# The split operands hhi, hlo, thi and tlo start 128 bytes later in every partition

## The chip, the cores and the metric

The kernel runs on one core of a Trainium2 chip. The metric is the device time of one execution in microseconds (us), taken as the median of 3 runs: 2562.43 us before the change (2559.01 to 2567.07).

TensorE multiplies, VectorE (DVE) and ScalarE (ACT) do the element-wise work, GpSimd (POOL) and SyncE (SP) mostly start transfers. The on-chip memory SBUF has 128 partitions. A tile has the same start in each of them, counted in bytes from the start of a partition; this document calls that number its address.

## The reference

Two layers of a decoder trunk work on a sequence of 1024 tokens with a model width of 1024, in float32. Each layer does, in this order:

```
h = rms_norm(x, norm1_w[l]) * (1.0 + sc1) + sh1
x = x + g1 * hybrid_mixer(h, w_in[l], w_out[l], ...)
h = rms_norm(x, norm2_w[l]) * (1.0 + sc2) + sh2
x = x + g2 * conv_ffn(h, w_gate[l], w_val[l], conv_w[l], conv_b[l], w_down[l])
```

The six vectors sh1 to g2 come from `silu(c) @ ada_w[l] + ada_b[l]`. The mixer projects h to 4096 columns, runs four retention heads and four gated linear recurrence (HGRN2) heads of 128 columns each, and projects back. Its lower bounds are `cumsum(softmax(hgrn_lb_logits)) - p[0]`, a handful of numbers per head. The gated MLP has 2816 columns and a causal convolution of width 3 on its gate branch. A last rms_norm ends it.

## The kernel before, in words

Every large product keeps float32 accuracy by splitting each operand in two numbers of the type float32r, a high and a low one, and adding three products: high by high, high weight by low operand, low weight by high operand. One such triple is lines 453 to 455 (`product`), 528 to 530 (`slot_mm`) or 368 to 370 (`gemm_half`). Each multiplication takes a weight tile of 128 x 128 and streams a moving tile of 128 x 512.

The moving tiles lie in four buffers. `hhi` and `hlo` hold the normalised input (2 halves x 8 slices x 512 columns each) or, in later stages, other operands; `thi` and `tlo` hold three sets of 4 slices for the Strassen-like scheme of `pair`, which makes the product of two blocks in seven multiplications of 4 triples. The weights arrive by DMA in `raw`, are split by ACT (line 330, `whi`) and DVE (line 331, `wlo`), and sit in six buffers of each kind. The moving buffers are filled by ACT (the high part: lines 311, 323, 414 and 533) and DVE (the low part: lines 312, 324, 415 and 534), most often from one of the twelve general tiles `z`.

Over the whole kernel there are 9360 of these 512-column multiplications: 5712 in `pair` (68 pairs of 84), 768 in plain units, 768 for the output projection `wo` and 2112 for `w_down`. Beside them TensorE does transposes and the small attention products, in plain float32 on tiles `z`.

The order of the work comes from the order in which the code is written and from priorities given to the scheduler. Addresses have no part in it. They come from the order in which a pool's tiles are asked for: each starts where the one before it ended, rounded up to 32 bytes. The pool `const` starts at 16512 and holds the twelve `z`, `ident`, `onec`, `hhi`, `hlo`, then small constants. Among these are `lbc`, `omlb`, `ex` and `sm`, 32 bytes each, which the function `bounds` fills once and the HGRN2 heads read as per-partition scalars. The pool `tops` opens when the input buffers of the start (`boot`) are given back, and takes their place from 179680 on: first a tile `shift` that nothing reads or writes, then `thi` and `tlo`.

Of the kernel before, what the change touches and what calls it, by code (L numbers as in the profile page):

```python
# [9 lines left out]
F32 = mybir.dt.float32  # L10
# [6 lines left out]
P = 128  # L17
# [3 lines left out]
DEPTH = 2  # L21
HEADS = 4
# [18 lines left out]
def kernel(  # L41
# [11 lines left out]
    const = ctx.enter_context(tc.tile_pool(name="const", bufs=1))  # L53
# [29 lines left out]
    onec = const.tile([P, 1], F32, name="onec")  # L83
    V.memset(onec, 1.0)

    hhi = const.tile([P, 2, KT, HALF], F32R, name="hhi")
    hlo = const.tile([P, 2, KT, HALF], F32R, name="hlo")
    b11, b12 = (hhi[:, 0, 0:4, :], hlo[:, 0, 0:4, :]), (hhi[:, 1, 0:4, :], hlo[:, 1, 0:4, :])
# [5 lines left out]
    def open_tops():  # L94
        boot.close()
        pool = ctx.enter_context(tc.tile_pool(name="tops", bufs=1, reuse_waits="tile"))
        pool.tile([P, 48], F32, name="shift")
        thi = pool.tile([P, 3, 4, HALF], F32R, name="thi")
        tlo = pool.tile([P, 3, 4, HALF], F32R, name="tlo")
        for i in range(3):  # L100
            tops[i + 1] = (thi[:, i], tlo[:, i])
# [669 lines left out]
    load_cols(1, vec_a, nc.scalar, zc)  # L771
    load_cols(2, vec_b, nc.scalar, zc)
    zc.free()
    lbc = const.tile([P, DEPTH * HEADS], F32, name="lbc")
    omlb = const.tile([P, DEPTH * HEADS], F32, name="omlb")
    ex = const.tile([P, DEPTH * HEADS], F32, name="ex")
    sm = const.tile([P, 8], F32, name="sm")
    first.turn()
    first.keep()
    ada_first(2)  # L780
# [4 lines left out]
    def start_units():  # L785
# [15 lines left out]
        ada_first(3)  # L801
        ada_first(1)
        open_tops()
        st.append(wcols(*parts[2], early=nc.sync))
        part(2, 0, lo)
# [342 lines left out]
```

## Time and profile before

| | |
|---|---|
| median of 3 runs | 2562.43 us |
| the profiled execution's own time | 2557.94 us |
| its span, first to last instruction | 2556.2 us |
| TensorE busy with multiplications | 2483.7 us, 97% of the span |
| TensorE loading weights | 2060.0 us, 81% |
| DVE busy | 1842.0 us, 72% |
| ACT busy | 999.5 us, 39% |
| mean granted TensorE clock | 0.986 of full speed |

The busy time of TensorE counts an instruction from its start to its modelled end, and one starts before the last has ended. So the time between two starts tells more than the duration of one.

### The profile page before, as it was taken

To read this page: it belongs to the slowest core of one execution; us is meant where nothing else is said; L and a number is where in the kernel's file an instruction comes from. 1 tells how busy PE (TensorE), PEld (TensorE's weight loads), DVE (VectorE), ACT (ScalarE), POOL (GpSimd) and SP (SyncE) were. 2 spreads that over 40 slices of the span, in tenths; PEclk is the share of its full clock that TensorE was granted. 3 is DMA by queue.
4 is the path that set the end of the run, shared out by engine and by line. 5 is a ranking of instruction groups with operands and counts; after the bars stand their busy time and mean duration, and the time that the engine had idled before them with its cause. 6 is when DMAs were issued, how large, how long until landed. Compare 5 with 4: busy or idle time off the path is not lost.

```text
span 2556.2 us, 32084 instructions
## 1 busy us (share of the span) xinstructions
PE 2483.7 (97%) x12189; PEld 2060.0 (81%) x12189; DVE 1842.0 (72%) x3045; ACT 999.5 (39%) x1685; POOL 78.3 (3%) x150
## 2 busy tenths in 40 slices
PE   6989999999999999999999999999999999999998
PEld 5778888778888888788888888887878888878887
DVE  6978888755988888734379788776398777773435
ACT  5533443434533333412264443344263333341224
POOL 0000000010000000000000000000000000000000
PEclk8989999999999999999999999999999999999999
DMA  8232332552234435733231211235212222264313
GB/s 306 66 104 83 99 108 72 181 181 79 83 124 148 140 124 165 252 111 97 86 114 58 67 59 42 67 99 161 87 58 83 75 91 83 75 215 133 97 56 109
DMA packets 293916, 283.52 MB, mean 111 GB/s; under 512 B 10794, under 2 KB 240770, under 8 KB 293762
## 3 DMA queue, kind: packets, MB, share of 16 engines
q1 hardware_dynamic: 275904, 219.42, 28.1%
q0 software_dynamic: 17408, 61.88, 6.7%
q8 instruction: 96, 1.57, 0.3%
q14 instruction: 59, 0.48, 0.1%
q10 hardware_dynamic: 449, 0.17, 0.0%
HBM read 229.00 MB, written 52.43 MB: 110 GB/s over the span
## 4 chain that ended last, share of the span: by engine, by line
PE 65%; issue 23%; DVE 5%; DMA 4%; ACT 1%; POOL 0%; SPq 0%; POOLq 0%; ACTq 0%; DVEq 0%
PE f L455 9%; PE f L453 9%; PE f L454 9%; PE dn L530 5%; PE dn L528 5%; PE dn L529 5%; PE wo L529 2%; PE wo L528 2%; PE wo L530 2%; PE dn_last L530 1%; PE dn_last L528 1%; PE dn_last L529 1%; DMA rawwo<-in_w_out_dram 1%; PE g L455 1%; PE g L454 1%
## 5 line engine op out<-in xcount | busy, mean ns | idle before, releaser
L455 PE MATMUL f<-hhi,wlof 128*128 128x512 f32 x640 | 251.6, 393 | 0.0
L453 PE MATMUL f<-hhi,whif 128*128 128x512 f32 x640 | 250.7, 392 | 0.6 <-DVE z L486 0.6
L454 PE MATMUL f<-hlo,whif 128*128 128x512 f32 x640 | 249.8, 390 | 0.0
L486 DVE TENSOR_TENSOR z<-z,f 128x512 f32<-128x512 f32 x240 | 164.2, 685 | 102.5 <-PE f L455 90.4
L455 PE MATMUL f<-thi,wlof 128*128 128x512 f32 x480 | 188.7, 393 | 0.0
L453 PE MATMUL f<-thi,whif 128*128 128x512 f32 x480 | 187.8, 391 | 0.0
L454 PE MATMUL f<-tlo,whif 128*128 128x512 f32 x480 | 187.3, 390 | 0.0
L530 PE MATMUL dn<-hhi,wlodn 128*128 128x512 f32 x384 | 151.9, 396 | 7.7 <-DVE wlodn L331 7.7
L528 PE MATMUL dn<-hhi,whidn 128*128 128x512 f32 x384 | 150.9, 393 | 0.0
L529 PE MATMUL dn<-hlo,whidn 128*128 128x512 f32 x384 | 150.3, 391 | 0.0
L919 DVE SCALAR_TENSOR_TENSOR z<-dn,mod,z 128x512 f32<-128x512 f32 x64 | 48.0, 750 | 134.5 <-PE dn L530 134.5
L454 PEld LDWEIGHTS f<-hlo,whif 128*128 128x128 f32 x640 | 120.2, 188 | 27.2
L453 PEld LDWEIGHTS f<-hhi,whif 128*128 128x128 f32 x640 | 120.2, 188 | 26.2 <-issue 0.9
L455 PEld LDWEIGHTS f<-hhi,wlof 128*128 128x128 f32 x640 | 120.2, 188 | 25.8
L168 DVE SCALAR_TENSOR_TENSOR ac<-aw,cact,ac 128x512 f32<-128x512 f32 x140 | 104.7, 748 | 23.6 <-DMA aw<-in_ada_w_dram 22.6
L330 ACT ACTIVATE whidn<-rawdn 128x512 fp32r<-128x512 f32 x64 | 39.6, 628 | 182.9 <-PE dn L529 171.3
L454 PEld LDWEIGHTS f<-tlo,whif 128*128 128x128 f32 x480 | 90.1, 188 | 20.6
L455 PEld LDWEIGHTS f<-thi,wlof 128*128 128x128 f32 x480 | 90.2, 188 | 19.3
L453 PEld LDWEIGHTS f<-thi,whif 128*128 128x128 f32 x480 | 90.2, 188 | 19.1
L530 PEld LDWEIGHTS dn<-hhi,wlodn 128*128 128x128 f32 x384 | 72.5, 189 | 24.2 <-DVE wlodn L331 8.5
L723 PEld LDWEIGHTS lh<-z,z 128*128 128x128 f32 x640 | 80.4, 198 | 10.6 <-issue 5.3
L529 PEld LDWEIGHTS dn<-hlo,whidn 128*128 128x128 f32 x384 | 72.5, 189 | 16.6
(659 smaller groups left out, 6348.3 us busy)
## 6 DMA issues: line engine op xcount, KB each, us to landing
aw<-in_ada_w_dram SPq DMA_DIRECT2D x160, 256.0 KB, 3.0
acts<-z POOLq DMA_DIRECT2D x44, 512.0 KB, 2.9
z<-acts SPq DMA_DIRECT2D x44, 512.0 KB, 4.3
z<-xd POOLq DMA_DIRECT2D x32, 512.0 KB, 5.8
rawdn<-in_w_down_dram SPq DMA_DIRECT2D x32, 512.0 KB, 4.3
xd<-z POOLq DMA_DIRECT2D x52, 256.0 KB, 2.7
rawdn_last<-in_w_down_dram SPq DMA_DIRECT2D x32, 384.0 KB, 3.6
af<-in_ada_w_dram SPq DMA_DIRECT2D x16, 512.0 KB, 9.8
```

Source lines behind the costliest of these rows:

```text
L168: V.scalar_tensor_tensor(out=a, in0=raw, scalar=cact[:, k:k + 1], in1=a, op0=ALU.mult, op1=ALU.add)
L330: A.activation(hi[:, 0:n], src, AF.Copy)
L453: T.matmul(ps, wh, rh, start=first and k == 0, stop=False, skip_group_check=True)
L454: T.matmul(ps, wh, rl, start=False, stop=False, skip_group_check=True)
L455: T.matmul(ps, wl, rh, start=False, stop=k == 3, skip_group_check=True)
L486: V.tensor_add(o, x, y)
L528: T.matmul(ps, a, rh, start=i == 0, stop=False)
L529: T.matmul(ps, a, rl, start=False, stop=False)
L530: T.matmul(ps, b, rh, start=False, stop=i == last)
L723: T.matmul(ps[:, c * 64:(c + 1) * 64].rearrange("p (b t) -> p b t", t=s), k.t[:, cs], qp.t[:, cs].rearrange("p (b t) -> p b t", t=s)[:, 1: ...
L919: V.scalar_tensor_tensor(out=x, in0=ps, scalar=mod[:, l * 48 + gate + d:][:, 0:1], in1=x, op0=ALU.mult, op1=ALU.add)
```

## The change

```
@@ -83,6 +83,10 @@
     onec = const.tile([P, 1], F32, name="onec")
     V.memset(onec, 1.0)
 
+    lbc = const.tile([P, DEPTH * HEADS], F32, name="lbc")
+    omlb = const.tile([P, DEPTH * HEADS], F32, name="omlb")
+    ex = const.tile([P, DEPTH * HEADS], F32, name="ex")
+    sm = const.tile([P, 8], F32, name="sm")
     hhi = const.tile([P, 2, KT, HALF], F32R, name="hhi")
     hlo = const.tile([P, 2, KT, HALF], F32R, name="hlo")
@@ -94,7 +98,7 @@
         pool = ctx.enter_context(tc.tile_pool(name="tops", bufs=1, reuse_waits="tile"))
-        pool.tile([P, 48], F32, name="shift")
+        pool.tile([P, 80], F32, name="shift")
         thi = pool.tile([P, 3, 4, HALF], F32R, name="thi")
         tlo = pool.tile([P, 3, 4, HALF], F32R, name="tlo")
@@ -771,10 +775,6 @@
     zc.free()
-    lbc = const.tile([P, DEPTH * HEADS], F32, name="lbc")
-    omlb = const.tile([P, DEPTH * HEADS], F32, name="omlb")
-    ex = const.tile([P, DEPTH * HEADS], F32, name="ex")
-    sm = const.tile([P, 8], F32, name="sm")
     first.turn()
```

Four constants of 32 bytes are asked for earlier, and the unused tile grows from 192 to 320 bytes. The table shows the addresses that follow, in bytes, and what is left of them after division by 128, 256, 512 and 1024.

| tile | address before | after | mod 128 | mod 256 | mod 512 | mod 1024 |
|---|---|---|---|---|---|---|
| hhi | 66208 | 66336 | 32, 32 | 160, 32 | 160, 288 | 672, 800 |
| hlo | 98976 | 99104 | 32, 32 | 160, 32 | 160, 288 | 672, 800 |
| thi | 179872 | 180000 | 32, 32 | 160, 32 | 160, 288 | 672, 800 |
| tlo | 204448 | 204576 | 32, 32 | 160, 32 | 160, 288 | 672, 800 |
| cact, mod, modA, cols0 to cols2 | 131744 to 133152 | 128 more | | | | |
| lbc, omlb, ex, sm | 133152 to 133280 | 66208 to 66336 | | | | |
| z0 to z11, ident | 16512 to 66176 | the same | 0 | 128 | 128 | 128 |
| raw, whi, wlo, aw, s1, ac | 134752 to 177760 | the same | 96 | 96 | 96 | 608 |

Slices of the moving buffers are 2048 bytes apart and slices of the weights 512 bytes, so all slices of a buffer have the same remainder by 512. All other tiles stay where they were, and the instructions, their order on every engine and their waits are the same in both kernels, apart from addresses.

## Rows read from the trace of the kernel before

**Rows 1.** The head of the profile page: the span, and each engine's busy time, its share of the span and its number of instructions.

```profile
span 2556.2 us, 32084 instructions
...
PE 2483.7 (97%) x12189; PEld 2060.0 (81%) x12189; DVE 1842.0 (72%) x3045; ACT 999.5 (39%) x1685; POOL 78.3 (3%) x150
```

**Rows 2.** The chain of work that ended last, its shares of the span by engine.

```profile
PE 65%; issue 23%; DVE 5%; DMA 4%; ACT 1%; POOL 0%; SPq 0%; POOLq 0%; ACTq 0%; DVEq 0%
```

**Rows 3.** Busy time of each engine in chosen stretches (us from the start): length, then busy us and number of instructions of PE, PEld (weight loads), DVE, ACT and POOL, the granted clock, the DMA share and GB/s.

```profile
34.00:36.60 2.60, 2.60 (x7) 1.98 (x6) 2.50 (x9) 2.57 (x6) 0.00 (x0) 0.50 1.05 384
...
1900.00:2200.00 300.00, 300.00 (x1312) 246.14 (x1312) 230.56 (x326) 116.41 (x168) 7.97 (x15) 1.00 0.25 80
```

**Rows 4.** TensorE's instructions in order of time, from a stretch at full clock in the output projection: start in us, duration in us, instruction.

```profile
1800.14 0.39 PE L530 MATMUL wo<-thi,wlowo 128*128 128x512 f32 x1
1800.37 0.39 PE L528 MATMUL wo<-thi,whiwo 128*128 128x512 f32 x1
1800.60 0.39 PE L529 MATMUL wo<-tlo,whiwo 128*128 128x512 f32 x1
...
1802.89 0.39 PE L530 MATMUL wo<-thi,wlowo 128*128 128x512 f32 x1
```

**Rows 5.** Groups of TensorE's multiplications, shapes kept apart: line, names, shapes, count, busy us and mean ns of one, idle time before them. They are the largest groups of each moving buffer.

```profile
L455 PE MATMUL f<-hhi,wlof 128*128 128x512 f32 x640 | 251.6, 393 | 0.0
L453 PE MATMUL f<-hhi,whif 128*128 128x512 f32 x640 | 250.7, 392 | 0.6 <-DVE z L486 0.6
L454 PE MATMUL f<-hlo,whif 128*128 128x512 f32 x640 | 249.8, 390 | 0.0
L455 PE MATMUL f<-thi,wlof 128*128 128x512 f32 x480 | 188.7, 393 | 0.0
L453 PE MATMUL f<-thi,whif 128*128 128x512 f32 x480 | 187.8, 391 | 0.0
L454 PE MATMUL f<-tlo,whif 128*128 128x512 f32 x480 | 187.3, 390 | 0.0
```

**Rows 6.** Groups of DVE, the same columns as rows 5. They differ in the buffers that they read and write.

```profile
L331 DVE TENSOR_TENSOR wlodn<-rawdn,whidn 128x512 fp32r<-128x512 f32 x64 | 43.7, 686 | 41.5 <-ACT whidn L330 41.5
L324 DVE TENSOR_TENSOR hlo<-z,hhi 128x512 fp32r<-128x512 f32 x52 | 35.0, 689 | 0.6
L415 DVE TENSOR_TENSOR tlo<-z,thi 128x512 fp32r<-128x512 f32 x48 | 32.8, 690 | 0.1
L432 DVE TENSOR_TENSOR z<-z,z 128x512 f32<-128x512 f32 x16 | 11.0, 690 | 0.0
L312 DVE SCALAR_TENSOR_TENSOR hlo<-t,mod,hhi 128x512 fp32r<-128x512 f32 x12 | 8.5, 748 | 0.0
L207 DVE SCALAR_TENSOR_TENSOR z<-af,cact,z 128x512 f32<-128x512 f32 x28 | 20.9, 747 | 0.0
L534 DVE TENSOR_TENSOR tlo<-z,thi 128x1024 fp32r<-128x1024 f32 x32 | 38.8, 1222 | 15.6 <-ACT thi L533 15.6
L534 DVE TENSOR_TENSOR hlo<-z,hhi 128x1024 fp32r<-128x1024 f32 x28 | 34.0, 1222 | 18.8 <-ACT hhi L533 18.6
L903 DVE TENSOR_TENSOR z<-z,z 128x1024 f32<-128x1024 f32 x16 | 19.6, 1222 | 4.9 <-ACT z L902 3.2 <-DMA z<-md 1.7
```

**Rows 7.** Groups of ACT, the same columns.

```profile
L330 ACT ACTIVATE whidn<-rawdn 128x512 fp32r<-128x512 f32 x64 | 39.6, 628 | 182.9 <-PE dn L529 171.3 <-DMA rawdn<-in_w_down_dram 9.7 <-PE dn L530 1.0
L323 ACT ACTIVATE hhi<-z 128x512 fp32r<-128x512 f32 x52 | 31.7, 624 | 0.6
L414 ACT ACTIVATE thi<-z 128x512 fp32r<-128x512 f32 x48 | 29.3, 628 | 10.6 <-DVE z L433 6.0 <-DVE z L430 4.0 <-DVE z L432 0.2
L533 ACT ACTIVATE thi<-z 128x1024 fp32r<-128x1024 f32 x32 | 33.5, 1059 | 30.2 <-DMA z<-acts 27.8 <-DVE z L903 1.4 <-PE g L455 0.6
L902 ACT ACTIVATE z<-z 128x1024 f32<-128x1024 f32 x16 | 16.9, 1059 | 6.3 <-DVE z L486 6.2
```

**Rows 8.** TensorE's instructions in order of time, the columns of rows 4, near the start, in the stretch of the first line of rows 3, at half clock.

```profile
34.07 0.63 PE L370 MATMUL uh_0f<-hhi,wloh_0f 128*128 128x512 f32 x1
34.50 0.63 PE L368 MATMUL uh_0f<-hhi,whih_0f 128*128 128x512 f32 x1
...
36.63 0.63 PE L368 MATMUL uh_0q<-hhi,whih_0q 128*128 128x512 f32 x1
```

**Rows 9.** The view and columns of rows 8, for two runs of plain float32 multiplications whose operands lie at other addresses: in kvh both are tiles z, in rb the moving tile is rTs (address 177888) and the weights are ident. Rows of one kind are merged: the duration is that of all of them together.

```profile
170.21 1.73 PE L555 MATMUL kvh<-z,z 128*128 128x128 f32 x14
46.15 1.12 PE L293 MATMUL rb<-rTs,ident 4*128 4x128 f32 x8 [0.46 <-DVE rTs L288]
```

**Rows 10.** The durations of one record of the two kinds in rows 9, over the whole run, from the views of the tiles kvh and rb: count, then minimum, median and maximum in ns, first and last start in us.

```profile
L555 PE MATMUL kvh<-z,z x112: 275/275/377, 170.2 to 1675.1; 128*128 128x128 f32 x112
...
L293 PE MATMUL rb<-rTs,ident x64: 270/270/421, 19.4 to 1870.4; 4*128 4x128 f32 x64
```

**Rows 11.** Weight loads of TensorE, the same columns as rows 5.

```profile
L453 PEld LDWEIGHTS f<-hhi,whif 128*128 128x128 f32 x640 | 120.2, 188 | 26.2 <-issue 0.9
L723 PEld LDWEIGHTS lh<-z,z 128*128 128x128 f32 x640 | 80.4, 198 | 10.6 <-issue 5.3 <-DVE z L715 1.3 <-PE h L455 1.2
```

More of the change, by code (lines that the diff above doesn't have):

```diff
@@ L84 @@
     V.memset(onec, 1.0)
+    lbc = const.tile([P, DEPTH * HEADS], F32, name="lbc")
+    omlb = const.tile([P, DEPTH * HEADS], F32, name="omlb")
+    ex = const.tile([P, DEPTH * HEADS], F32, name="ex")
+    sm = const.tile([P, 8], F32, name="sm")
     hhi = const.tile([P, 2, KT, HALF], F32R, name="hhi")
@@ L96, in open_tops @@
         pool = ctx.enter_context(tc.tile_pool(name="tops", bufs=1, reuse_waits="tile"))
-        pool.tile([P, 48], F32, name="shift")
+        pool.tile([P, 80], F32, name="shift")
         thi = pool.tile([P, 3, 4, HALF], F32R, name="thi")
@@ L773 @@
     zc.free()
[L774 to L777, printed above, removed]
     first.turn()
```

## The prediction

> **What bounds the kernel now.** I read the head of the page first. TensorE is busy for 97% of the span, DVE for 72%, ACT for 39% [rows 1]. The chain that ended last says the same in another way: 65% of it is TensorE's own work and 23% is "issue", where the engine waits for nothing that the profile shows, while DVE has 5% and DMA 4% [rows 2]. So the time is set by how fast TensorE takes its instructions, hardly by anyone it waits for. The table by stretches makes this sharper: in the 300 us from 1900 on there is no idle time, the granted clock is 1.00, and 1312 multiplications run [rows 3]. They start 300 / 1312 = 0.2287 us apart. The order in time, from another stage, gives (1802.89 - 1800.14) / 12 = 0.229 us between starts [rows 4]. The "mean ns" of 390 to 393 [rows 5] is a duration with an overlapping end, and the reader should not multiply by it.
>
> This step of 229 ns matters because there are 9360 of these 512-column multiplications: 9360 x 0.229 = 2143 us, 84% of the span of 2556.2. All of them stream a moving tile from hhi, hlo, thi or tlo. The change touches nothing but where these four buffers start, so the question is whether the step of 229 ns hangs on that. One nanosecond per step is 9.36 us.
>
> **The change, part by part.** It removes no instruction, adds none, moves none and adds no wait; SP's and POOL's queues hold the same transfers to the same places, since no transfer writes a tile that moved. What changes is addresses, and each user of a moved tile is a term.
>
> The four constants lbc, omlb, ex and sm, and the columns behind hlo: they are operands of one number per partition, or tiles of at most 108 columns written once. I put them at nothing. Should one of these small accesses cost more, it is DVE's or ACT's, and both stand idle for a good part of the span [rows 1].
>
> DVE and ACT filling the four buffers: here the trace does show several places. DVE's subtraction takes 686 ns where source, second source and result lie in the weight buffers (all 96 mod 256), 689 and 690 ns where they lie in z (128) and the moving buffers (160), and 690 ns where all lie in z [rows 6]. The form with a scalar takes 748 ns with t (96) and hhi (160), 747 with af (224) and z (128). With 1024 columns it is 1222 for thi, for hhi and for z alone. ACT takes 628 for a weight buffer, 624 for hhi, 628 for thi, and 1059 for thi and for z with 1024 columns [rows 7]. These rows differ by at most 0.7%, and the larger one isn't tied to a place. The distances between operands that they show, modulo 256, are 0, 32, 64 and 96; the new distance between z and hhi is 160, which no row has. If it cost another 0.7%, DVE's splits of rows 6 (35.0 + 32.8 + 8.5 + 38.8 + 34.0 = 149 us) would grow by 1 us, beside TensorE's work. Term: 0, bounds -1 and +1 us.
>
> TensorE reading the moving tiles: the one large term. What can the trace say? Of the address modulo 1024, hhi and thi have the same remainder (672), so that rows of hhi and of thi agree to within 3 ns [rows 5] says only that the bits above that do not matter. Remainders modulo 512 other than 160 never occur for these multiplications, so the new place is not shown. Three things bear on it.
>
> First, at half clock (0.50 of 2.4 GHz, so 1.2 GHz [rows 3]) the step is (36.63 - 34.07) / 6 = 0.4267 us [rows 8], which is 512 cycles of 1.2 GHz: one column per cycle and nothing on top. At full clock the columns alone are then half of that, 213.3 ns, and the step of 229 carries 15.6 ns more. If the place of the operand caused this excess, and the new place caused none, the change would be worth 9360 x 15.6 ns = 146 us. That is the bound below.
>
> The Trainium skill puts a number on the same step: its page "TensorE: Matmul & The Clock Gate", section "Wait — 56ns, not 53.3ns?", states 512 columns at full clock as 512 / 2.4 plus about 2.5 ns, 215.7 measured. The trace does not agree: 229. If the page's step were to be had by another address, the gain would be 9360 x 13.3 = 124 us (an estimate from the page), and if it holds for other operand types only, nothing.
>
> Second, plain float32 multiplications with other places: kvh, where weights and moving tile are both z and so have a distance of 0 modulo 256, starts every (1.73 - 0.275) / 13 = 0.112 us. For rb, whose moving tile (177888, so 224 modulo 256) lies 96 from its weights (128), I get (1.12 - 0.27) / 7 = 0.121 [rows 9], with the median of one record taken off as the tail [rows 10]. The difference, 9 ns, is the most that a row shows between two places, and rb has four partitions only and starts after an idle time, which alone may explain it. Taken as it is and per instruction, 9360 x 9.4 ns = 88 us, the bound above.
>
> Third, the weight loads: 188 ns where the weights are float32r (whif), 198 where they are z [rows 11]; both fit in 229, so the load would have to grow by 41 ns before it set the step.
>
> I take 0 for this term, nearest to the rows of DVE and ACT, which read the same buffers at the same places. The excess appears at 2.4 GHz and is absent at 1.2 GHz with the very same addresses, so it looks like a limit on how fast things are taken, not like a collision.
>
> **The sum.** 0 us on the execution of 2557.94 us (span 2556.2 and 1.7 around it). The median of the three runs is 2562.43, 4.5 above it, so the unchanged time to forecast is the median: 2562 us. The three runs span 8 us, and about 0.3%, 7.7 us, is what a measurement of this kernel can tell from no change; it is 0.82 ns per step. The forecast's own range is 2552 to 2572.
>
> **Rivals.**
>
> A, the excess goes: the new place (32 modulo 256 in place of 160) spares some of the 15.6 ns, as a read that meets fewer collisions with the weights would. For it: the excess is unexplained, and of the four places modulo 512 that leave 32 modulo 128 only one was seen. Against it: the step is the same 229 for all four weight slices and for hhi as for thi. Anything from 0.82 to 15.6 ns is open; half of it, 7.8 ns, makes 73 us: 2489 us.
>
> B, the slow side: the moving read and the weight load that runs beneath it come into each other's way at a distance of 192 bytes modulo 512 where they did not at 64. Its place is every one of the 9360 steps, and it decides from 0.82 ns per step. For it: weight loads run through 81% of the span [rows 1], so the two reads are always on at once, and rb's 9 ns. Against it: kvh at distance 0, where the operands should meet most, is the quicker one [rows 9]. Half of rb's difference, 4.7 ns, makes 44 us: 2606 us.
>
> The Trainium skill speaks against both: "SBUF — State Buffer", section "Who interferes with whom", lets only DVE and GpSimd share a port and says that TensorE never waits on anyone. No run here has shown it for another place.
>
> C, DVE or ACT becomes dearer at distance 160 and TensorE is held up. For it: DVE is 72% busy. Against it: rows 6 and 7. At 0.7% of 149 us it would give 2563 us, which is the forecast again.
>
> **How the numbers follow.** Forecast 0.54, A 0.27, B 0.19, with C inside the forecast. Of the forecast I leave 0.02 to a median that falls low by chance and 0.01 to one that falls high: faster by over 0.3% 0.29, within 0.3% 0.51, slower 0.20. For 8 in 10 the range must take in about half of A and of B: down by 9360 x 8.3 ns = 78 us, up by 9360 x 5.3 ns = 50 us, so 2484 to 2612. With gains of all sizes up to 15.6 ns alike likely this holds 0.53 of A, and 0.57 of B up to 9.4 ns.
>
> **What would show it.** Right: in the stretch from 1900 to 2200 us again about 1312 multiplications with no idle time, f, dn and wo at 390 to 396 ns, starts 0.229 us apart at full clock and 0.427 at half. A shows itself as more than 1316 in such a stretch, B as fewer than 1307 (0.82 ns is 0.36% of a step). C would leave the step at 0.229 and show DVE's rows L324, L415 and L534 longer and TensorE idle behind them. The forecast is wrong if the step is anything but 229, since no other term has weight.

## The result and the profile after

The changed kernel takes 2588.63 us (median of 4 runs, 2588.16 to 2589.55) against 2560.72 for the kernel before on the same chip (4 runs, 2558.01 to 2567.07): 1.0106 times as long, 95% interval 1.0086 to 1.0126. So 128 bytes of layout cost 27.9 us. The forecast was no change; the time lies inside the range, on the side of rival B.

The head of the page, the chain's shares and the stretch from 1900 us on, as in [rows 1], [rows 2] and [rows 3]:

```profile
span 2586.4 us, 32084 instructions
...
PE 2520.2 (97%) x12189; PEld 2060.0 (80%) x12189; DVE 1847.3 (71%) x3045; ACT 999.6 (39%) x1685; POOL 78.8 (3%) x150
...
PE 51%; issue 39%; DMA 4%; DVE 4%; ACT 1%; POOL 1%; SPq 0%; POOLq 0%; ACTq 0%; DVEq 0%
```

```profile
32.00:35.00 3.00, 3.00 (x9) 2.28 (x8) 2.93 (x8) 2.97 (x7) 0.00 (x0) 0.50 1.06 387
1900.00:2200.00 300.00, 300.00 (x1287) 241.72 (x1286) 231.50 (x327) 116.91 (x170) 7.98 (x15) 1.00 0.24 78
```

The whole loss stands in the first line: TensorE's busy time grew by 2520.2 - 2483.7 = 36.5 us, while the time in which it did not multiply fell from 72.5 (2556.2 - 2483.7) to 66.2 us. The span grew by the difference, 30.2 us. The stretch without idle time shows where it sits: 1287 multiplications in 300 us in place of 1312, 0.2331 us from one to the next in place of 0.2287, at the same full clock. In the chain, TensorE's own work and "issue" make 90% together, where they made 88% before; only the split between the two is another. TensorE's instructions in order of time, at full clock and in the stretch at half clock near the start, as in [rows 4] and [rows 8]:

```profile
1830.20 0.40 PE L532 MATMUL wo<-hhi,whiwo 128*128 128x512 f32 x1
1830.44 0.39 PE L533 MATMUL wo<-hlo,whiwo 128*128 128x512 f32 x1
...
1833.71 0.39 PE L532 MATMUL wo<-thi,whiwo 128*128 128x512 f32 x1
```

```profile
32.73 0.63 PE L374 MATMUL uh_0f<-hhi,wloh_0f 128*128 128x512 f32 x1
33.16 0.63 PE L372 MATMUL uh_0f<-hhi,whih_0f 128*128 128x512 f32 x1
...
34.87 0.63 PE L374 MATMUL uh_0q<-hhi,wloh_0q 128*128 128x512 f32 x1
```

Fifteen steps from 1830.20 to 1833.71 make 0.234 us each. Five steps from 32.73 to 34.87 make 0.428. Over all steps between 420 and 435 ns, those at half clock, the mean was 426.7 ns before and is 426.6 now: at half clock the new place costs nothing.

The groups of TensorE, DVE and ACT that answer to [rows 5], [rows 6] and [rows 7] (the line numbers of early code are 4 higher):

```profile
L457 PE MATMUL f<-hhi,whif 128*128 128x512 f32 x640 | 253.7, 396 | 0.5 <-DVE z L490 0.5
L459 PE MATMUL f<-hhi,wlof 128*128 128x512 f32 x640 | 253.1, 395 | 0.0
L458 PE MATMUL f<-hlo,whif 128*128 128x512 f32 x640 | 253.1, 395 | 0.0
L457 PE MATMUL f<-thi,whif 128*128 128x512 f32 x480 | 190.1, 396 | 0.0
```

```profile
L328 DVE TENSOR_TENSOR hlo<-z,hhi 128x512 fp32r<-128x512 f32 x52 | 34.8, 684 | 0.6
L419 DVE TENSOR_TENSOR tlo<-z,thi 128x512 fp32r<-128x512 f32 x48 | 32.4, 682 | 0.0
L436 DVE TENSOR_TENSOR z<-z,z 128x512 f32<-128x512 f32 x16 | 10.8, 682 | 0.0
L538 DVE TENSOR_TENSOR tlo<-z,thi 128x1024 fp32r<-128x1024 f32 x32 | 38.7, 1219 | 14.6 <-ACT thi L537 14.5
```

```profile
L327 ACT ACTIVATE hhi<-z 128x512 fp32r<-128x512 f32 x52 | 31.6, 622 | 0.6
L418 ACT ACTIVATE thi<-z 128x512 fp32r<-128x512 f32 x48 | 28.9, 623 | 9.2 <-DVE z L437 5.0 <-DVE z L434 4.0
```

In the groups shown the duration of a multiplication rose by 2 to 5 ns, about as much as the step; since it overlaps with the next one, only the step may be multiplied by a count. The rows of DVE and ACT that use the moved buffers did not get longer; L419 fell from 690 to 682 ns, and so did L436, whose operands did not move, so that is no effect of the place. DVE's busy time is 5.3 us higher than before all the same: it counts overlapping instructions once, and they overlap less. The durations of its instructions, added up, fell from 2018.4 to 2012.8 us.

### The profile page after: what moved, and what is told of

It is laid out like the page before. It is cut to its first block, busy times and chain, and to the rows that moved or that the text cites. A ratio compares the mean times of both kernels' runs of the same rounds, so it can differ in the third digit from the quotient of the medians.

```text
span 2586.4 us, 32084 instructions
## 1 busy us (share of the span) xinstructions
PE 2520.2 (97%) x12189; PEld 2060.0 (80%) x12189; DVE 1847.3 (71%) x3045; ACT 999.6 (39%) x1685; POOL 78.8 (3%) x150
## 4 chain that ended last, share of the span: by engine, by line
PE 51%; issue 39%; DMA 4%; DVE 4%; ACT 1%; POOL 1%; SPq 0%; POOLq 0%; ACTq 0%; DVEq 0%
PE f L459 5%; PE f L457 5%; PE f L458 5%; PE dn L534 5%; PE dn L532 5%; PE dn L533 5%; PE wo L532 2%; PE wo L534 2%; PE wo L533 2%; PE g L458 1%; PE g L457 1%; PE g L459 1%; PE dn_last L532 1%; PE dn_last L534 1%; PE dn_last L533 1%
## 5 line engine op out<-in xcount | busy, mean ns | idle before, releaser
L534 PE MATMUL dn<-hhi,wlodn 128*128 128x512 f32 x384 | 152.5, 397 | 6.8 <-DVE wlodn L335 6.8
L534 PEld LDWEIGHTS dn<-hhi,wlodn 128*128 128x128 f32 x384 | 72.3, 188 | 25.3 <-DVE wlodn L335 7.6
L533 PEld LDWEIGHTS dn<-hlo,whidn 128*128 128x128 f32 x384 | 72.2, 188 | 17.6
```

What stands on the lines that cost most here:

```text
L533: T.matmul(ps, a, rl, start=False, stop=False)
L534: T.matmul(ps, b, rh, start=False, stop=i == last)
```

## The experiments

All kernels compute the whole function, with the same instructions in the same order as the kernel before; only addresses differ. Two measures are used: the time, and the mean distance between the starts of neighbouring 512-column multiplications, over all such distances up to 245 ns in a trace ("step"). Where a step is given for one kind of moving buffer, hhi and hlo or thi and tlo, both neighbours read that kind. Each trace is of one execution. The step of the kernel before is 229.0 ns, that of the changed one 233.3. Where a run has one timing only, its time is that of a single execution.

**One part of the change alone.** In hhi_only the four constants are moved and the pad, the unused tile `shift`, stays at 192 bytes; in thi_only the pad alone is changed.

```
 # hhi_only: the constants in front of hhi as in the changed kernel, and
         pool.tile([P, 48], F32, name="shift")
 # thi_only: the constants where they were, and
-        pool.tile([P, 48], F32, name="shift")
+        pool.tile([P, 80], F32, name="shift")
```

> The four constants are laid out first, so hhi and hlo start at 66336 and 99104 (32 modulo 256); thi and tlo stay at 179872 and 204448 (160 modulo 256). If the step between two multiplications hangs on where their own moving tile lies, steps that stream hhi or hlo take 233.3 ns as in the changed kernel and steps that stream thi or tlo 229.0 as before: 5376 of the 9360 steps, so 57% of the 28 us, 2577 us. If only the tops buffers matter the time is that of before, 2561; if only hhi and hlo do, 2588.

> Only the unused tile in front of thi grows to 320 bytes; hhi and hlo stay at 160 modulo 256. By the same theory thi and tlo steps take 233.3 ns and the others 229.0: 3984 of 9360 steps, 43% of 28 us, 2573 us. The two runs together must make the whole 28 us; if they do not, the place of one buffer alone is not the cause.

Measured: hhi_only 2571.93 us, 1.0054 of the kernel before (1.0038 to 1.0069); thi_only 2568.14 us, 1.0040 (1.0022 to 1.0057); the kernel before, timed beside them, took 2558.20. In hhi_only the steps of hhi and hlo are 233.1 ns and those of thi and tlo 229.1; in thi_only it is 229.1 and 233.0. The stretch without idle time has multiplications of both kinds, and both counts lie between 1287 and 1312:

```profile
1900.00:2200.00 300.00, 300.00 (x1298) 243.54 (x1297) 232.32 (x329) 117.13 (x169) 8.52 (x16) 1.00 0.25 81
```

```profile
1900.00:2200.00 300.00, 300.00 (x1302) 244.37 (x1301) 229.96 (x326) 115.67 (x167) 7.98 (x15) 1.00 0.25 79
```

The first is hhi_only, the second thi_only. Each part of the change has its own share, and each buffer is slow by itself. The two times add to 13.7 + 9.9 = 24 of the 28 us, within the intervals of the three ratios.

**Own place or distance.** Here, starting from the changed kernel, the weights move too, by 128 bytes, and the smaller pad leaves thi and tlo where the change put them.

```
+    stg.tile([P, 32], F32, name="pads", bufs=1)
...
-        pool.tile([P, 80], F32, name="shift")
+        pool.tile([P, 48], F32, name="shift")
```

> The changed kernel's moving buffers (32 modulo 256), and raw, whi, wlo and the tiles behind them 128 bytes later too, so that the distance from weights to moving tile is 64 bytes modulo 256 again as before. Theory own place: the step stays at 233.3 ns and the time at 2588 us. Theory distance (the moving read and the weight load beneath it meet): the step is 229.0 again and the time 2561 us.

Measured: 2556.19 us, 0.9997 of the kernel before (0.9977 to 1.0017), a step of 229.1 ns. The head of the page and the stretch of this run are nearly those of the kernel before (2483.7 us busy and 1312 multiplications):

```profile
PE 2483.9 (97%) x12189; PEld 2061.1 (81%) x12189; DVE 1842.1 (72%) x3045; ACT 998.4 (39%) x1685; POOL 78.3 (3%) x150
```

```profile
1900.00:2200.00 300.00, 300.00 (x1312) 246.18 (x1311) 230.15 (x323) 114.14 (x163) 8.51 (x16) 1.00 0.26 82
```

The moving buffers lie where they are slow, and the kernel is fast. Own place falls: what counts is where the moving tile lies in relation to the weights.

**A map with many distances at once.** Beside the edit shown, there are 32 unused bytes in front of hlo, none in front of thi and 96 in front of tlo.

```
-        hi = stg.tile([P, HALF], F32R, tag="whi", bufs=NW, name=f"whi{nm}")
-        lo = stg.tile([P, HALF], F32R, tag="wlo", bufs=NW, name=f"wlo{nm}")
+        hi = stg.tile([P, HALF + 8], F32R, tag="whi", bufs=NW, name=f"whi{nm}")
+        lo = stg.tile([P, HALF + 8], F32R, tag="wlo", bufs=NW, name=f"wlo{nm}")
```

> Each of the twelve weight buffers is 32 bytes longer than its tile, so that they start at 128, 160, ... 480 modulo 512, one after the other; hhi lies at 160, hlo at 192, thi at 128 and tlo at 224 modulo 256. Own place: the step is the same for all twelve weight buffers and differs between the four moving ones, 229.0 for hhi. Distance: within each moving buffer the step differs from weight buffer to weight buffer, between about 229 and 233.3 ns or beyond, and depends on moving minus weight address alone.

Measured: 2577.18 us. The trace does not name the buffers of the weights; they follow from the order in which the six of a kind are used, and the distance here is that to the weights loaded while the tile streams. The step differs from weight buffer to weight buffer, which own place does not allow, between 230.9 and 234.7 ns. But it is no function of the distance alone: at one distance (224 modulo 512) it was 234.7 for hlo and 232.5 for thi, and no pair came down to the 229.0 that distance 64 has elsewhere. Where every multiplication has another distance than its neighbours, the steps do not separate. So the next runs give every weight buffer the same distance, and one distance to hhi and hlo and another to thi and tlo.

**The map, two distances per run.** D is the moving tile's address minus that of the weights. Unused bytes in front of the weights (S) and in front of thi (shift) set it: D = 64 - S for hhi and hlo, 384 + shift for thi and tlo, modulo 512. For d32_d384 this is

```
+    stg.tile([P, 8], F32, name="pads", bufs=1)
...
-        pool.tile([P, 48], F32, name="shift")
```

and the others have S and shift of 64 and 32 (d0_d416), 96 and 224 (d480_d96), 128 and 256 (d448_d128), 64 and 384 (d0_d256), 64 and 448 (d0_d320).

> From here on D is the address of the moving tile minus that of the weights, modulo 512: 64 in the kernel before, 192 in the changed one. Here D is 32 for hhi and hlo and 384 for thi and tlo, by 32 unused bytes in front of the weights and none in front of thi. Theory distance: each of the two kinds has one step of its own, set by D. If the pattern repeats every 128 bytes, 64 and 192 would have had the same step, which they have not; if every 256, the step at 384 is that at 128 in another run of this set. Rival: only the very place of the kernel before is good, and every other D gives 233.3 ns.

> D is 0 for hhi and hlo and 416 for thi and tlo. Theory distance: if the two reads collide because they meet at the same place, D = 0 should be the worst, well above 233.3 ns; if collisions only shift along the stream, it lies between 229 and 234.

> D is 480 for hhi and hlo and 96 for thi and tlo. Theory distance: 96 lies between 64 (229.0) and 192 (233.3), so the step lies between them if the cost grows evenly with the distance; a step below 229.0 in either kind would be a better layout than that of the kernel before.

> D is 448 for hhi and hlo and 128 for thi and tlo. With a period of 256 bytes, 448 has the step of 192, 233.3 ns, and 128 that of 384 in the run before; with a period of 512 they are free.

> hhi and hlo at D = 0, thi and tlo at D = 256. With a period of 256 bytes both kinds take 227.8 ns; with one of 512 the second is free.

> hhi and hlo at D = 0, thi and tlo at D = 320, which is 64 modulo 256. With a period of 256 bytes the second kind takes 229.0 ns as in the kernel before, with one of 512 it is free.

| run | time, us | D of hhi, hlo: step, ns | D of thi, tlo: step, ns |
|---|---|---|---|
| d32_d384 | 2587.47 | 32: 233.2 | 384: 232.7 |
| d0_d416 | 2563.38 | 0: 227.8 | 416: 234.0 |
| d480_d96 | 2582.84 | 480: 233.2 | 96: 233.6 |
| d448_d128 | 2579.45 | 448: 233.4 | 128: 232.2 |
| d0_d256 | 2537.02 | 0: 227.3 | 256: 227.3 |
| d0_d320 | 2549.21 | 0: 228.3 | 320: 229.6 |
| before | 2560.72 | 64: 229.1 | 64: 229.0 |
| changed | 2588.63 | 192: 233.3 | 192: 233.3 |

The first six rows are single executions, four on one chip and two on another, and the kernel before alone took between 2548.98 and 2569.25 us in its runs; so the times rank the layouts only roughly, and the reading rests on the steps. The one execution of the kernel before beside the first four took 11712.72 us, which fits no other run and is not used.

The two levels can be read off the order in time of d0_d416, in one product of hhi and hlo and the one of thi and tlo in front of it:

```profile
2008.74 0.40 PE L454 MATMUL f<-thi,whif 128*128 128x512 f32 x1
...
2016.94 0.40 PE L456 MATMUL f<-thi,wlof 128*128 128x512 f32 x1
2017.17 0.40 PE L454 MATMUL f<-hhi,whif 128*128 128x512 f32 x1
...
2027.84 0.39 PE L456 MATMUL f<-hhi,wlof 128*128 128x512 f32 x1
```

The 35 steps from 2008.74 to 2016.94 take 0.2343 us each, the 47 from 2017.17 to 2027.84 take 0.2270. Distances 256 apart have nearly the same step: 0 and 256, 64 and 320, 128 and 384, 192 and 448. So the period is 256 bytes as far as it was tried. Meeting at the same place is not the worst but the best: 0 gives 227.3 to 228.3, 64 gives 229.0 to 229.6, and the six others (32, 96, 128, 160, 192, 224 modulo 256) lie between 232.2 and 234.0. Both guesses on the shape fell: D = 0 is not slow, and 96 does not lie between 64 and 192. So did the rival that only the place before is good.

**A better layout.** All at D = 0.

```
+    stg.tile([P, 16], F32, name="pads", bufs=1)
...
-        pool.tile([P, 48], F32, name="shift")
+        pool.tile([P, 32], F32, name="shift")
```

> All four moving buffers at D = 0 modulo 512 (64 unused bytes in front of the weights, 128 in front of thi). In the run d0_d416 the steps of hhi and hlo at D = 0 were 227.8 ns against 229.0 before. Theory distance: the step is 227.8 throughout, 1.2 ns less on 9360 steps, 11 us less than the kernel before, about 2548. Rival: the 227.8 ns came from the neighbours thi and tlo at 416, and the step here is 229.0 and the time that of before.

Measured: 2540.84 us, 0.9931 of the kernel before (0.9906 to 0.9956), a step of 227.3 ns. It beats both kernels, by 0.7% and by 1.8%. The gain on the kernel before is 17.6 us (2558.47 beside it) and not the 11 expected, since the step fell by 1.8 ns and not by 1.2. The stretch and the head of the page:

```profile
1900.00:2200.00 300.00, 300.00 (x1326) 248.39 (x1325) 229.92 (x323) 111.96 (x159) 8.51 (x16) 1.00 0.26 82
```

```profile
PE 2467.7 (97%) x12189; PEld 2058.6 (81%) x12189; DVE 1840.5 (72%) x3045; ACT 999.2 (39%) x1685; POOL 78.1 (3%) x150
```

**Which weights.** D = 0 from whi and 480 from wlo; in front of the weights lie 64 unused bytes, in front of thi 96.

```
+    padw = []
...
+        if not padw:
+            padw.append(stg.tile([P, 8], F32, tag="padw", bufs=1, name="padw"))
         lo = stg.tile([P, HALF], F32R, tag="wlo", bufs=NW, name=f"wlo{nm}")
```

> All four moving buffers at D = 0 from the high weights whi, and at D = 480 (224 modulo 256) from the low weights wlo, by 32 unused bytes between the two. While a moving tile streams, the weights of the multiplication behind it are loaded: wlo while hlo or tlo streams, whi while hhi or thi does. If the stream meets that load, steps of hlo and tlo take 233.2 ns and steps of hhi and thi 227.3. If it meets its own weights, the steps of hhi and thi with wlo are long and those with whi short. If only the sum over a triple is set, all three are alike, near 229.2.

Measured: 2581.97 us. Steps of hlo and tlo take 238.3 ns, those of hhi and thi with whi 232.5, those with wlo 228.7. The order in time, with the weight loads (PEld) between, shows which load runs under which multiplication:

```profile
2003.43 0.40 PE L458 MATMUL f<-hhi,whif 128*128 128x512 f32 x1
2003.43 0.19 PEld L459 LDWEIGHTS f<-hlo,whif 128*128 128x128 f32 x1
2003.66 0.40 PE L459 MATMUL f<-hlo,whif 128*128 128x512 f32 x1
2003.66 0.19 PEld L460 LDWEIGHTS f<-hhi,wlof 128*128 128x128 f32 x1
2003.90 0.39 PE L460 MATMUL f<-hhi,wlof 128*128 128x512 f32 x1
2003.90 0.19 PEld L458 LDWEIGHTS f<-thi,whif 128*128 128x128 f32 x1
2004.13 0.40 PE L458 MATMUL f<-thi,whif 128*128 128x512 f32 x1
```

The long step is the one under which wlo is loaded, and the step of the multiplication that uses wlo is the shortest: the delay goes with the load for the multiplication behind, not with a tile's own weights. The recorded load itself does not get longer (188 ns in this run and in the kernel before); it is the next start that comes late. How the two reads get into each other's way inside the memory is not visible in a trace.

The sizes came out otherwise than expected. Over the 227.3 ns of D = 0, the step with the load of wlo has 11.0 ns more, but the step before it has 5.2 more and the one behind it 1.4. The three steps sum to 699.5 ns, as much as three steps at a distance of 224 modulo 256 (3 x 233.2), although only one load in three has that distance. Why one wrong load in three costs as much as three, and why part of it shows one step early, is not settled.

## Why the prediction was wrong

**What bounds the kernel** held. The step of the 512-column multiplications set the time before and after, and the change acted through nothing else.

**The term "TensorE reading the moving tiles"** is the step that failed. It was put at 0, "nearest to the rows of DVE and ACT, which read the same buffers at the same places". That nearness was no evidence: DVE and ACT load no weights, and what counts here is the distance of the moving tile from the weights that TensorE loads meanwhile. The term measured +4.3 ns per step. On 9360 steps that would be 40 us. The steps of up to 245 ns, 8871 before and 8865 after, add up to 36.4 us more than before (2068.4 against 2032.0), and TensorE's busy time grew by 36.5, so hardly anything else in it grew; 6.3 us came back as less idle time.

**The reasoning behind the 0** failed in one sentence: the excess "is absent at 1.2 GHz with the very same addresses, so it looks like a limit on how fast things are taken, not like a collision." At half clock the changed kernel shows no excess either (426.6 ns), and at full clock the excess does depend on addresses. That an effect hides at the slower clock says nothing on whether it hangs on the place.

**Rival B** had the right mechanism and the right place: the moving read and the weight load beneath it, at 192 bytes in place of 64. Its price, 4.7 ns per step against 4.3 measured, came close by luck: it was half of a difference between two rows that differ in more than the distance, and no row gave a reason for the half. Its time of 2606 us was 17 us too high: 0.4 ns too much per step makes 4 of them, and most of the rest is what the idle time and the steps not at full clock gave back. What spoke against it, that kvh "at distance 0, where the operands should meet most, is the quicker one" [rows 9], was read the wrong way round: distance 0 is the best there is. That row agreed with the map, but was taken as speaking against B.

**Rival A** was not what the change did, but a smaller form of it exists. The excess over 213.3 ns was 15.6 ns before; D = 0 removes 1.8 of it, and at least 14 ns stay at every distance tried. What the prediction held against it, the same 229 ns for all weight slices and for hhi as for thi, could not speak either way: all of these had the one distance of 64. Rival **C** fell: L324, L415 and L534 (now L328, L419 and L538) got no longer, and TensorE's idle time did not grow.

The Trainium skill's page "TensorE: Matmul & The Clock Gate", section "Step-by-step: what each phase is for", says that TensorE's two read ports are independent and that loading the next weights takes no read bandwidth from the running multiplication. The runs do not agree: the step moves between 227.3 and 234.0 ns with the distance between the two reads, and in split_w it is above all the step over the misplaced load that grows.

## What to carry to other kernels

When a kernel is bound by TensorE at full clock, the distance in SBUF between the streamed operand and the weights is a tuning size of its own: here it was worth up to 3% of a step, and a multiple of 256 bytes was best. A tile that is asked for earlier or later moves everything behind it, so after any change of layout the distance between starts should be compared in a stretch without idle time, before anything else is blamed. Rows of other engines, and rows at half clock, do not tell whether the place matters.

## What was not expected of the hardware

- With float32r operands of 128 x 512 and 128 x 128, the step at full clock was 227.3 to 228.3 ns at D = 0 modulo 256, 229.0 to 229.6 at 64, and 232.2 to 234.0 at 32, 96, 128, 160, 192 and 224. At half clock it was 427 ns before and after the change.
- 64 bytes are good while 32 and 96 are not; no rule for that was found, and distances that are no multiple of 32 were not tried.
- Neighbouring steps are coupled: with the distances mixed (map1, split_w) the steps are not those that the single distances give.
